# Gate and up products of a two-layer trunk as seven quadrant products on one Trainium2 core

## The chip, the core and the metric

The kernel runs on one core of a Trainium2 chip. The metric is the device time of one execution in microseconds. Before the change three runs gave 1435.06, 1439.13 and 1439.5 us, a median of 1439.13 us.

## What is computed

The reference is a decoder trunk of two layers with 512 tokens, width 1024 and float32 data. Each layer has a mixer (retention and a state space model in layer 0, differential attention in layer 1), then a feed-forward part and a gated embedding. The change is in the feed-forward part, which has 2816 hidden columns:

```python
def swiglu(h, w_gate, w_up, w_down):
    return (jax.nn.silu(h @ w_gate) * (h @ w_up)) @ w_down
```

It is called once per layer on the normalised `h` of 512 x 1024.

## The kernel before

The trunk is written through a framework that schedules the instructions at build time: a timeline model there fixes one order for each engine and puts in the semaphores. On the chip each engine then takes its instructions in that order, so one that waits holds up all behind it on its engine. Buffers come from pools; a new tile waits until an earlier tile's last reader has released a slot.

A float32 product is made of three products of parts in the format float32r. A cast on ScalarE writes the high part (`hi`, line 98), a subtraction on VectorE the low part (`lo`, line 101), and `mm3` (lines 120 to 122) adds hi x hi, hi x lo and lo x hi in PSUM. The normalised activations are kept transposed, as `xh` and `xl` of 128 x 8 x 512 (eight pieces of 128 rows of the width, 512 tokens).

`ffn` (from line 965) goes over 22 tiles of 128 hidden columns. For each it loads 1024 columns of gate and of up weights (`gu`, two DMAs of 512 KB), splits them into `whi` and `wlo`, and `gu_mm` makes 2 outputs x 8 pieces x 3 = 48 matmuls of 512 columns into two PSUM banks. Then ScalarE takes the silu of the gate bank (line 993), VectorE multiplies it with the up bank into `pr` (line 994), and a split gives `ah` and `al`. For the first two tiles the matmuls come in two halves of 256 columns, so that they can begin before all tokens are normalised. After `FA` = 12 tiles and after the last, the down product (`gemm_nat`, 512 columns) adds what these tiles give to the residual (`residual_evac`, line 245):

```python
            if ft in (FA - 1, NFT - 1):
                half = 0 if ft == FA - 1 else 1
                prs = range(6) if half == 0 else range(6, 11)
                nt = open_norm(i_out) if half else None
                for c in range(2):
                    gemm_nat(ah, al, [A["down"][L, c, i] for i in prs], [2] * len(prs),
                             residual_evac(i_out, c, half == 1, nt if c else None), t_outer=(half == 1 and c == 1))
```

The pools of `whi` and `wlo` have five slots each, that of the raw weights three. PSUM has six banks for products here.

Of the kernel before, what the change touches and what calls it, by code (L numbers as in the profile page):

```python
# [9 lines left out]
F32 = mybir.dt.float32  # L10
F32R = mybir.dt.float32r
BF16 = mybir.dt.bfloat16
I32 = mybir.dt.int32
AF = mybir.ActivationFunctionType
ALU = mybir.AluOpType
# [4 lines left out]
P = 128  # L20
D = 1024
S = 512
NT = S // P
KD = D // P
FH = 2816
NFT = FH // P
FA = 12
EPS = 1e-6
MAGIC = 12582912.0
TWO_PI = 2.0 * math.pi  # L30
# [36 lines left out]
def trunk(ctx: ExitStack, tc, A, out, stop=None, tap=None):  # L67
    nc = tc.nc
    V, G, AC, PE, SP = nc.vector, nc.gpsimd, nc.scalar, nc.tensor, nc.sync

    cpool = ctx.enter_context(tc.tile_pool(name="cpool", bufs=1))
    wpool = ctx.enter_context(tc.tile_pool(name="wpool", bufs=5))
    rpool = ctx.enter_context(tc.tile_pool(name="rpool", bufs=3))
# [12 lines left out]
    def f(t):  # L86
        return t.bitcast(F32)

    def bank(tag="mm"):
        r = rings[tag]  # L90
        n = r[0] + r[2] % r[1]
        r[2] += 1
        n, w = (f"b{n // 2}", 2) if n < 6 else (f"c{n}", 1)
        return psum.tile([P, 512], F32, tag=n, name=n, bufs=w)

    def split(hi, lo, src, hi_eng=AC, lo_eng=V):
        if hi_eng is AC:
            AC.copy(out=hi, in_=src)  # L98
        else:
            hi_eng.tensor_copy(out=hi, in_=src)  # L100
        lo_eng.tensor_tensor(out=lo, in0=src, in1=f(hi), op=ALU.subtract)  # L101
# [3 lines left out]
    def wload(ap, lo_eng=V, parts=1):  # L105
        if on_pool[0] > 0:
            on_pool[0] -= 1
            lo_eng = G
        raw = rpool.tile([P, 1024], F32, tag="raw", name="raw")
        hi = wpool.tile([P, 1024], F32R, tag="whi", name="whi")  # L110
        lo = wpool.tile([P, 1024], F32R, tag="wlo", name="wlo")
        w = 1024 // parts
        for i in range(parts):
            cs = slice(i * w, (i + 1) * w)
            SP.dma_start(out=raw[:, cs], in_=ap[:, cs])
            split(hi[:, cs], lo[:, cs], raw[:, cs], lo_eng=lo_eng)
# [41 lines left out]
    def norm_fn(i, gain, alloc, tr=lambda t: "tr"):  # L158
        def scaled(t):
            rstd_of(i, t)  # L160
            y = alloc()
            for c in range(2):
                V.scalar_tensor_tensor(out=y[c], in0=hold[0][:, t, c * 512:(c + 1) * 512], scalar=rst[:, i, t:t + 1],
                                       in1=gain[c], op0=ALU.mult, op1=ALU.mult)
            return y

        def norm_t(t):
            y = scaled(t)
            for c in range(2):
# [22 lines left out]
    def gemm_parts(xh, xl, pieces, kpp, evac, k0=0, lo_engs=(V,), last=(), ring="mm"):  # L192
        w = [wload(a, lo_engs[i % len(lo_engs)]) for i, a in enumerate(pieces)]
        wk = []
        for (hi, lo), n in zip(w, kpp):
            for j in range(n):
                wk.append((hi[:, j * 512:(j + 1) * 512], lo[:, j * 512:(j + 1) * 512]))
        n = len(wk)

        order = [k for k in range(n) if k not in last] + list(last)  # L200

        def part(t, ring=ring, *cols):
            b = bank(ring)
# [38 lines left out]
    def residual_evac(i, c, do_sq=True, after=None):  # L242
        def ev(t, b):
            hs = hold[0][:, t, c * 512:(c + 1) * 512]
            V.tensor_tensor(out=hs, in0=b, in1=hs, op=ALU.add)
            if do_sq:
                sumsq(i, t, c)
            if after is not None:
                after(t)
        return ev  # L250
# [702 lines left out]
    def gu(L, ft):  # L953
        return bank(), bank(), [wload(A["gateup"][L, ft, i]) for i in range(2)]

    def gu_mm(w, a, b):
        for o, (whi, wlo) in zip(w[:2], w[2]):
            for k in range(KD):
                cs = slice(k * P, (k + 1) * P)
                mm3(o[:, a:b], whi[:, cs], wlo[:, cs], xh[:, k, a:b], xl[:, k, a:b], k == 0, k == KD - 1)  # L960
# [8 lines left out]
    def ffn(L, i_in, i_out, pre=None):  # L969
        banks(mm=6, tr=2)  # L970
        st = ExitStack()
        fp = st.enter_context(tc.tile_pool(name=f"ffn{L}", bufs=1, side="right"))
        if pre is None:
            close_norm()
            first, rest = ffn_first(L, 0, 256), (256, 512)
        else:
            first, rest = pre, (0, 256)
            rings["mm"][2] = 4
        ah = al = None
        for ft in range(NFT):  # L980
            if ft in (0, FA):
                ah = fp.tile([P, FA, S], F32R, tag="ah", name="ah")
                al = fp.tile([P, FA, S], F32R, tag="al", name="al")
            if ft < 2:
                w = first[ft]
                gu_mm(w, *rest)
            else:
                w = gu(L, ft)
                gu_mm(w, 0, 512)
            gb, ub = w[:2]  # L990
            sg = fp.tile([P, 512], F32, tag="sg", name="sg", bufs=2)
            pr = fp.tile([P, 512], F32, tag="pr", name="pr", bufs=2)
            AC.activation(sg, gb, AF.Silu)
            V.tensor_tensor(out=pr, in0=ub, in1=sg, op=ALU.mult)  # L994
            fi = ft % FA
            split(ah[:, fi], al[:, fi], pr)
            if ft in (FA - 1, NFT - 1):
                half = 0 if ft == FA - 1 else 1
                prs = range(6) if half == 0 else range(6, 11)
                nt = open_norm(i_out) if half else None  # L1000
                for c in range(2):
                    gemm_nat(ah, al, [A["down"][L, c, i] for i in prs], [2] * len(prs),
                             residual_evac(i_out, c, half == 1, nt if c else None), t_outer=(half == 1 and c == 1))
        st.close()

    def ple(L, i_in, i_out):
# [171 lines left out]
```

## Time and profile before

| | before |
|---|---|
| median of three runs | 1439.13 us |
| the profiled execution | 1437.59 us |
| its span, first to last instruction | 1435.8 us |
| TensorE (PE) busy | 1382.5 us, 96% |
| VectorE (DVE) busy | 723.0 us, 50% |
| ScalarE (ACT) busy | 553.5 us, 39% |
| GpSimd (POOL) busy | 276.8 us, 19% |
| mean granted TensorE clock | 0.976 |
| HBM traffic over the span | 99 GB/s |

The profiled execution has its own time, 1437.59 us, which is 1.8 us above its span. Matmuls are pipelined, so the duration of one is longer than the distance from its start to the next start; a rate is read from starts. PEld is the load of the stationary operand, which runs beside PE. DVE, ACT and POOL rows have true starts, and the bracket at the end of a timeline row tells how long the engine was idle before it and who ended that.

### The profile page before, as it was taken

What the parts mean: (1) busy time and instruction counts of PE and PEld (TensorE: products, weight loads), DVE (VectorE), ACT (ScalarE), POOL (GpSimd) and SP (SyncE); (2) the same over time, 40 slices, a digit from 0 to 9 for tenths busy, and PEclk for the clock granted to TensorE, in tenths of its full rate; (3) what the DMA queues carried; (4) which work ended last, traced back from release to release, by engine and by line L of the source; (5) the groups of instructions that cost most, each with busy time, mean ns of one, the idle gap of its engine ahead of it and who ended that gap; (6) DMA issues with size and microseconds to landing.
All of it is one profiled execution on the core that took longest, in us unless ns stands there. A gap on an engine that the chain in (4) does not pass through costs nothing.

```text
span 1435.8 us, 17051 instructions
## 1 busy us (share of the span) xinstructions
PE 1382.5 (96%) x6538; PEld 1131.3 (79%) x6538; DVE 723.0 (50%) x1244; ACT 553.5 (39%) x956; POOL 276.8 (19%) x275
## 2 busy tenths in 40 slices
PE   7999887899999999999999999898999999999997
PEld 5788665689888888888888888787988888888886
DVE  7998565454333233333553777887533323333344
ACT  5335445443232222222544565864423212232244
POOL 0113463331000000000344364732100000000041
PEclk9999788999999999999999999999999999999999
DMA  7532125324323333231432332323333332323241
GB/s 255 159 99 83 48 68 160 117 64 129 102 88 99 92 91 100 89 101 61 151 124 77 104 86 55 100 81 103 118 96 96 90 101 88 102 90 91 85 147 59
DMA packets 48272, 145.28 MB, mean 101 GB/s; under 512 B 10752, under 2 KB 10896, under 8 KB 48192
## 3 DMA queue, kind: packets, MB, share of 16 engines
q1 hardware_dynamic: 43040, 136.37, 30.0%
q0 software_dynamic: 5008, 7.84, 2.3%
q8 instruction: 51, 0.84, 0.2%
q14 instruction: 29, 0.24, 0.1%
q10 hardware_dynamic: 144, 0.00, 0.0%
HBM read 133.21 MB, written 8.88 MB: 99 GB/s over the span
## 4 chain that ended last, share of the span: by engine, by line
PE 87%; DVE 6%; issue 3%; ACT 2%; DMA 2%; POOL 1%; SPq 0%; POOLq 0%; ACTq 0%; DVEq 0%
PE b L120 26%; PE b L121 26%; PE b L122 26%; DVE wlo L101 1%; PE c L172 1%; DVE T L404 1%; PE c L853 1%; PE b L831 1%; PE b L830 1%; PE c L583 1%; ACT whi L98 0%; PE b L844 0%; PE c L609 0%; DMA raw<-in_xT_dram 0%; PE b L781 0%
## 5 line engine op out<-in xcount | busy, mean ns | idle before, releaser
L98 ACT CAST whi<-raw 128x1024 fp32r<-128x1024 f32 (+1 forms) x217 | 226.4, 1045 | 540.5 <-PE b L121 316.5
L101 DVE TENSOR_TENSOR wlo<-raw,whi 128x1024 fp32r<-128x1024 f32 (+1 forms) x192 | 239.3, 1248 | 330.8 <-ACT whi L98 326.7
L120 PE MATMUL b<-xh,whi 128*128 128x512 f32 (+1 forms) x800 | 300.7, 378 | 5.3 <-ACT whi L98 5.3
L121 PE MATMUL b<-xl,whi 128*128 128x512 f32 (+1 forms) x800 | 301.3, 378 | 0.0
L122 PE MATMUL b<-xh,wlo 128*128 128x512 f32 (+1 forms) x800 | 299.2, 377 | 0.0
L120 PE MATMUL b<-whi,xh 128*128 128x512 f32 (+1 forms) x576 | 228.8, 403 | 14.8 <-ACT xh L98 8.6
L121 PE MATMUL b<-wlo,xh 128*128 128x512 f32 (+1 forms) x576 | 230.9, 403 | 3.2 <-DVE wlo L101 3.2
L122 PE MATMUL b<-whi,xl 128*128 128x512 f32 (+1 forms) x576 | 226.7, 399 | 0.0
L120 PEld LDWEIGHTS b<-xh,whi 128*128 128x128 f32 x800 | 150.6, 189 | 35.9 <-ACT whi L98 5.7
L121 PEld LDWEIGHTS b<-xl,whi 128*128 128x128 f32 x800 | 151.1, 189 | 30.2
L122 PEld LDWEIGHTS b<-xh,wlo 128*128 128x128 f32 x800 | 150.8, 189 | 30.2
L125 POOL TENSOR_TENSOR rst<-ms,mhalf 128x1 f32<-128x1 f32 (+1 forms) x25 | 14.9, 599 | 782.6 <-DVE ms L154 734.1
L120 PEld LDWEIGHTS b<-whi,xh 128*128 128x128 f32 x576 | 110.6, 192 | 41.0 <-ACT xh L98 9.1
L121 PE MATMUL b<-wlo,ah 128*128 128x512 f32 x352 | 139.2, 395 | 0.0
L122 PE MATMUL b<-whi,al 128*128 128x512 f32 x352 | 138.9, 395 | 0.0
L120 PE MATMUL b<-whi,ah 128*128 128x512 f32 x352 | 138.7, 395 | 0.0
L121 PEld LDWEIGHTS b<-wlo,xh 128*128 128x128 f32 x576 | 111.0, 193 | 28.1 <-DVE wlo L101 4.5
L122 PEld LDWEIGHTS b<-whi,xl 128*128 128x128 f32 x576 | 109.9, 191 | 22.8 <-issue 0.5
L994 DVE TENSOR_TENSOR pr<-b,sg 128x512 f32<-128x512 f32 x44 | 30.5, 692 | 152.3 <-PE b L122 142.7
L121 PEld LDWEIGHTS b<-wlo,ah 128*128 128x128 f32 x352 | 66.0, 187 | 16.1
L120 PEld LDWEIGHTS b<-whi,ah 128*128 128x128 f32 x352 | 66.0, 187 | 16.0
L122 PEld LDWEIGHTS b<-whi,al 128*128 128x128 f32 x352 | 66.0, 187 | 16.0
(291 smaller groups left out, 1684.2 us busy)
## 6 DMA issues: line engine op xcount, KB each, us to landing
raw<-in_gateup_dram SPq DMA_DIRECT2D x88, 512.0 KB, 3.5
raw<-in_down_dram SPq DMA_DIRECT2D x44, 512.0 KB, 3.5
raw<-in_w_qkv_dram SPq DMA_DIRECT2D x24, 512.0 KB, 3.7
raw<-in_w_in_dram SPq DMA_DIRECT2D x19, 512.0 KB, 4.3
raw<-in_ple_gate_dram SPq DMA_DIRECT2D x16, 512.0 KB, 3.6
pj<-raw SPq DMA_DIRECT2D x8, 512.0 KB, 2.9
raw<-in_w_out_dram SPq DMA_DIRECT2D x8, 512.0 KB, 4.2
pj<-pj SPq DMA_DIRECT2D x8, 512.0 KB, 6.6
```

The lines of the kernel that those rows point to most:

```text
L98: AC.copy(out=hi, in_=src)
L101: lo_eng.tensor_tensor(out=lo, in0=src, in1=f(hi), op=ALU.subtract)
L120: PE.matmul(o, lhsT=sh, rhs=mh, start=start, stop=False)
L121: PE.matmul(o, lhsT=sh, rhs=ml, start=False, stop=False)
L122: PE.matmul(o, lhsT=sl, rhs=mh, start=False, stop=stop)
L125: G.tensor_tensor(out=dst, in0=src, in1=mhalf[:, :w], op=ALU.pow)
L172: PE.transpose(out=b[:, j * P:(j + 1) * P], in_=y[c][:, j * P:(j + 1) * P], identity=ident)
L404: TT = lambda e, o, a, b, op: e.tensor_tensor(out=o, in0=a, in1=b, op=op)
L583: PE.matmul(vb[:, g * 64:(g + 1) * 64], lhsT=AT[:, g], rhs=U[:, g], start=True, stop=True)
L830: PE.matmul(so, lhsT=QQ[m][:, qs], rhs=KK[m][:, 0:n], start=True, stop=False)
L831: PE.matmul(so, lhsT=QQ[m][:, qs], rhs=KZ[m][:, 0:n], start=False, stop=True)
L994: V.tensor_tensor(out=pr, in0=ub, in1=sg, op=ALU.mult)
```

## The change

Tiles 0, 1 and 2 of each layer stay as they were. From tile 3 (`NORD` = 3) on, gate and up of a tile are computed as one product of two 2 x 2 block matrices, in Winograd's form of Strassen's algorithm. The token matrix is cut into two halves of 256 tokens and two halves of the width (`x11`, `x12`, `x21`, `x22`); the weights into gate and up (columns) and two halves of the width (`b11`, `b21`, `b12`, `b22`). Seven products of 4 pieces x 3 = 12 matmuls with 256 columns each take the place of the 48 with 512.

- `x_sums`, once per layer, makes the sums S1 to S4 of token quadrants: ten VectorE operations on 128 x 1024 and four splits. S3 is written over `x21`, which tiles 0 to 2 still read.
- `w_sums`, once per tile, makes four sums of weight quadrants (T1 to T4, 128 x 512 each) and splits the plain weights `w1`, the pairs `w2` (T1, T2) and `w4` (T4 and b22), each 128 x 1024, and `w3` (T3, 128 x 512).
- Running sums are kept in PSUM: three copies by ScalarE (`s1`, `u2`, `u3`) save what a bank half holds at that moment, and three VectorE operations on 128 x 256 add them in elsewhere.
- The last two of a tile's seven products (`d_gate`, `d_up`) are issued within the next tile's.
- The down product comes after 8, 16 and 22 tiles (8, 8 and 6) where it came after 12 and 22.

```diff
-FA = 12
+FA = 8
+NORD = 3
...
+        def x_sums():
...
+            tt(s12, f(x21[0]), f(x22[0]), ALU.add)
+            tt(s12, s12, f(x21[1]), ALU.add)
+            tt(s12, s12, f(x22[1]), ALU.add)
+            put("S1", s12)
+            tt(s12, s12, f(x11[0]), ALU.subtract)
+            tt(s12, s12, f(x11[1]), ALU.subtract)
+            put("S2", s12)
+            tt(s3, f(x11[0]), f(x21[0]), ALU.subtract)
+            tt(s3, s3, f(x11[1]), ALU.add)
+            tt(s3, s3, f(x21[1]), ALU.subtract)
+            s4 = quad(fp.tile([P, 1024], F32, tag="T", name="s4"))
+            tt(s4, f(x12[0]), s12, ALU.subtract)
+            tt(s4, s4, f(x12[1]), ALU.add)
+            put("S4", s4)
+            return lambda: put("S3", s3, x21)
+
+        def w_sums(ft):
+            r1 = rpool.tile([P, 1024], F32, tag="raw", name="raw")
+            r2 = r2_tile("r2")
+            for r, i in ((r1, 0), (r2, 1)):
+                SP.dma_start(out=r, in_=A["gateup"][L, ft, i])
+            T = fp.tile([P, 1536], F32, tag="T", name="T")
...
+            w1 = pair(r1, wt())
+            tt(t1, b12, b11, ALU.subtract)
+            tt(t2, b22, t1, ALU.subtract)
+            w2 = pair(T[:, 0:1024], wt())
+            tt(t3, b22, b12, ALU.subtract)
+            w3 = pair(t3, [fp.tile([P, 512], F32R, tag=n, name=n, bufs=2) for n in ("t3h", "t3l")])
+            tt(b12, b21, t2, ALU.subtract)
+            w4 = pair(r2, wt())
...
+        def prod(o, w, x, start):
+            for k in range(HK):
+                cs = slice(k * P, (k + 1) * P)
+                for i, (wi, xi) in enumerate(((0, 0), (1, 0), (0, 1))):
+                    PE.matmul(o, lhsT=w[wi][:, cs], rhs=x[xi][:, k], start=start and k == 0 and i == 0,
+                              stop=k == HK - 1 and i == 2, skip_group_check=True)
+
+        def snap(src, n):
+            d = fp.tile([P, HS], F32, tag=n, name=n, bufs=2)
+            AC.copy(out=d, in_=src)
+            return d
...
+            def d_gate():
+                prod(X, w["T4"], x22, False)
+
+            def d_up():
+                prod(Y, w["22"], xs["S4"], False)
+                tt(Y, s["u2"], Y, ALU.add)
+                evac(ft, gb, ub)
...
+        for ft in range(NFT + 1):
+            if ft < NORD:
...
+                if ft == 1:
+                    put_s3 = x_sums()
+                if ft == NORD - 1:
+                    put_s3()
+                continue
...
+                prod(X, w["11"], x11, True)
+                s1 = snap(X, "s1")
+                prod(Z, w["21"], x12, True)
+                tt(gb[:, 0:HS], s1, Z, ALU.add)
+                if pend:
+                    pend[0]()
+                prod(X, w["T2"], xs["S2"], False)
+                u2 = snap(X, "u2")
+                if pend:
+                    pend[1]()
+                prod(Y, w["T1"], xs["S1"], True)
+                prod(X, w["T3"], xs["S3"], False)
+                u3 = snap(X, "u3")
+                tt(Z, u3, Y, ALU.add)
+                pend = finish_ft(ft, w, gb, ub, {"u2": u2}, None)
+            if ft == NFT or ft % FA == 0:
+                down(ft - 1 - (ft - 1) % FA, ft)
```

Three places of the built order follow. First VectorE in the middle of the tiles, before the change: one tile has four instructions (its product `pr`, its low part `al` and the low parts `wlo` of two later weight loads; `b` is a PSUM bank, `sg` the silu).

```order
L994 TENSOR_TENSOR pr<-b_3133,sg 128x512
L101 TENSOR_TENSOR wlo<-raw,whi 128x1024
L101 TENSOR_TENSOR al<-pr,ah 128x512
L101 TENSOR_TENSOR wlo<-raw,whi 128x1024
L994 TENSOR_TENSOR pr<-b_3201,sg 128x512
```

The same place with the change. A tile has thirteen; here stand twelve that follow the first weight sum T1 of one tile. `r` holds the up weights, `s`, `u` are the copies from PSUM, and `t3l` is the low part of T3.

```order
L986 TENSOR_TENSOR T<-r_3555 128x512
L986 TENSOR_TENSOR T<-r_3555,T 128x512
L102 TENSOR_TENSOR wlo<-r_3429,whi 128x1024
L986 TENSOR_TENSOR r_3555<-raw,T 128x512
L986 TENSOR_TENSOR b_3202<-u_3254,b_3202 128x256
L102 TENSOR_TENSOR wlo<-raw,whi 128x1024
L986 TENSOR_TENSOR pr<-b_3202,sg 128x512
L986 TENSOR_TENSOR b_3328<-u_3425,b_3328 128x256
L102 TENSOR_TENSOR t3l<-T,t3h 128x512
L986 TENSOR_TENSOR b_3453<-s_3467,b_3454 128x256
L102 TENSOR_TENSOR al<-pr,ah 128x512
L102 TENSOR_TENSOR wlo<-T,whi 128x1024
```

The four instructions of a tile have become thirteen: three of 1024 columns, six of 512 between SBUF tiles, `pr`, and three of 256 in PSUM.

Second, VectorE of the changed kernel at the passage from tile 2 to tile 3 in layer 0. `xl<-s3` is the low part of S3, `pr_2948` belongs to tile 2, `wlo_2967` and `wlo_2977` are the pairs w2 and w4 of tile 3, `wlo_3056` the plain weights w1 of tile 4.

```order
L102 TENSOR_TENSOR xl_79<-s3_2861,xh_78 128x4x256
L986 TENSOR_TENSOR r2_2956<-raw_2955,T_2959 128x512
L102 TENSOR_TENSOR t3l_2972<-T_2959,t3h_2971 128x512
L986 TENSOR_TENSOR pr_2948<-b2_2886,sg_2947 128x512
L102 TENSOR_TENSOR wlo_2967<-T_2959,whi_2966 128x1024
L102 TENSOR_TENSOR wlo_2977<-r2_2956,whi_2976 128x1024
L102 TENSOR_TENSOR wlo_3056<-raw_3050,whi_3055 128x1024
```

Six instructions, among them the low parts that TensorE needs next, stand behind the low part of S3. In layer 1 ten stand between it and the low part of w2 there.

Third, TensorE of the changed kernel at the same place, with its waits: the end of the second product of tile 3, then the first matmuls of tile 4.

```order
L1046 MATMUL b0_2981<-xl_79,whi_2960 128x256
L1046 MATMUL b1_3075<-xh_78,whi_3055 128x256 [waits PE_49,Activation_49]
L1046 MATMUL b1_3076<-xh_78,whi_3055 128x256 [waits DVE_49]
L1046 MATMUL b1_3075<-xh_78,wlo_3056 128x256 [waits DVE_49]
```

The 26 matmuls up to there (24 of tile 3, two of tile 4) need the plain weights alone; the next one waits for VectorE's `wlo_3056`.

## Rows read from the trace of the kernel before

**Rows 1.** The page: busy time by engine, and the chain that ended last.
```profile
PE 1382.5 (96%) x6538; PEld 1131.3 (79%) x6538; DVE 723.0 (50%) x1244; ACT 553.5 (39%) x956; POOL 276.8 (19%) x275
...
PE 87%; DVE 6%; issue 3%; ACT 2%; DMA 2%; POOL 1%; SPq 0%; POOLq 0%; ACTq 0%; DVEq 0%
```
**Rows 2.** Busy time by stretch: us; PE, PEld, DVE, ACT, POOL; clock; DMA share; GB/s.
```profile
400.00:450.00 50.00, 50.00 (x217) 40.55 (x216) 17.50 (x19) 14.43 (x18) 0.00 (x0) 1.00 0.31 95
450.00:500.00 50.00, 50.00 (x216) 40.23 (x215) 15.10 (x15) 10.53 (x11) 0.00 (x0) 1.00 0.30 87
```
**Rows 3.** Timeline of DVE over one tile: start us, duration us, what, idle before.
```profile
367.02 0.69 DVE L994 TENSOR_TENSOR pr<-b,sg 128x512 f32<-128x512 f32 x1 [3.52 <-PE b L122]
367.80 1.23 DVE L101 TENSOR_TENSOR wlo<-raw,whi 128x1024 fp32r<-128x1024 f32 x1
368.94 0.69 DVE L101 TENSOR_TENSOR al<-pr,ah 128x512 fp32r<-128x512 f32 x1
373.43 1.23 DVE L101 TENSOR_TENSOR wlo<-raw,whi 128x1024 fp32r<-128x1024 f32 x1 [3.80 <-ACT whi L98]
378.18 0.69 DVE L994 TENSOR_TENSOR pr<-b,sg 128x512 f32<-128x512 f32 x1 [3.52 <-PE b L122]
```
**Rows 4.** Timeline of PE in tile 1's half of 256 columns, twenty starts apart.
```profile
338.63 0.28 PE L122 MATMUL b<-xh,wlo 128*128 128x256 f32 x1
...
341.01 0.28 PE L121 MATMUL b<-xl,whi 128*128 128x256 f32 x1
```
**Rows 5.** Timeline of PEld in the same stretch.
```profile
338.52 0.19 PEld L122 LDWEIGHTS b<-xh,wlo 128*128 128x128 f32 x1
338.64 0.19 PEld L120 LDWEIGHTS b<-xh,whi 128*128 128x128 f32 x1
```
**Rows 6.** Groups by line, 300 to 690 us: count, busy us, mean ns, idle before.
```profile
L101 DVE TENSOR_TENSOR wlo<-raw,whi 128x1024 fp32r<-128x1024 f32 x60 | 73.5, 1225 | 141.5 <-ACT whi L98 139.7
L98 ACT CAST whi<-raw 128x1024 fp32r<-128x1024 f32 x67 | 70.3, 1050 | 241.9 <-PE b L121 155.6 <-PE b L122 67.3 <-issue 9.4
...
L994 DVE TENSOR_TENSOR pr<-b,sg 128x512 f32<-128x512 f32 x22 | 15.2, 692 | 80.2 <-PE b L122 71.2 <-ACT sg L993 9.0
L101 DVE TENSOR_TENSOR al<-pr,ah 128x512 fp32r<-128x512 f32 x22 | 15.1, 685 | 0.0
...
L98 ACT CAST ah<-pr 128x512 fp32r<-128x512 f32 x22 | 13.7, 621 | 0.0
...
L993 ACT ACTIVATE sg<-b 128x512 f32<-128x512 f32 x22 | 13.0, 592 | 0.0
```
**Rows 7.** Groups by line, 800 to 1000 us: 256 columns out of PSUM.
```profile
L857 DVE TENSOR_TENSOR vn<-c,vn 128x256 f32<-128x256 f32 x16 | 6.7, 418 | 8.8 <-ACT vn L856 8.8
...
L856 ACT COPY vn<-c 128x256 f32<-128x256 f32 x16 | 5.9, 369 | 16.4 <-PE c L854 16.4
```
**Rows 8.** Timeline of DVE where its instructions stand close, 93 to 107 us.
```profile
93.95 1.22 DVE L101 TENSOR_TENSOR wlo<-raw,whi 128x1024 fp32r<-128x1024 f32 x1
95.08 1.22 DVE L404 TENSOR_TENSOR Am<-BA,LM 128x1024 f32<-128x1024 f32 x1
...
105.42 0.68 DVE L404 TENSOR_TENSOR E<-bh,c 128x512 f32<-128x512 f32 x1
106.03 0.68 DVE L101 TENSOR_TENSOR vl<-b,vh 128x512 fp32r<-128x512 f32 x1
106.63 0.47 DVE L238 SCALAR_TENSOR_TENSOR rt<-b,rst,c 128x256 f32<-128x256 f32 x1
107.02 0.47 DVE L239 SCALAR_TENSOR_TENSOR rt<-b,rst,c 128x256 f32<-128x256 f32 x1
```
**Rows 9.** Timeline of DVE: the product `pr` of tile 2, layer 0 and layer 1.
```profile
355.87 0.69 DVE L994 TENSOR_TENSOR pr<-b,sg 128x512 f32<-128x512 f32 x1 [3.52 <-PE b L122]
...
1044.69 0.69 DVE L994 TENSOR_TENSOR pr<-b,sg 128x512 f32<-128x512 f32 x1 [3.57 <-PE b L122]
```
**Rows 10.** Busy time by stretch around a pause of PE in layer 0's mixer.
```profile
264.00:270.00 6.00, 2.69 (x11) 1.57 (x9) 5.56 (x5) 4.86 (x6) 5.96 (x4) 1.00 0.15 25
270.00:280.00 10.00, 7.93 (x28) 6.25 (x29) 6.24 (x6) 3.58 (x6) 2.61 (x2) 0.66 0.73 252
```

More of the change, by code (lines that the diff above doesn't have):

```diff
@@ L978, in ffn @@
             rings["mm"][2] = 4
[L979 to L986, printed above, removed]
-            else:
[L988 to L1003, printed above, removed]
@@ new lines, in ffn, with tt, r2_tile, put @@
+        HK, HS = KD // 2, S // 2
+        lo_t, hi_t = slice(0, HS), slice(HS, S)
+        x11, x12, x21, x22 = ([x[:, a:a + HK, t] for x in (xh, xl)] for t in (lo_t, hi_t) for a in (0, HK))
+        xs = {}
+        def tt(o, a, b, op):
+            V.tensor_tensor(out=o, in0=a, in1=b, op=op)
+        def r2_tile(name):
+            return fp.tile([P, 1024], F32, tag="r2", name=name, bufs=2)
+        def x_sums():
+            quad = lambda x: x.rearrange("p (k n) -> p k n", k=HK)
+            def put(n, src, dst=None):
+                if dst is None:
+                    dst = [fp.tile([P, HK, HS], F32R, tag=f"{n}{i}", name=f"{n}{i}") for i in "hl"]
+                split(dst[0], dst[1], src)
+                xs[n] = dst
+            s12, s3 = quad(r2_tile("s12")), quad(r2_tile("s3"))
+            tt(s12, f(x21[0]), f(x22[0]), ALU.add)
[13 more added lines that the diff above has]
+            return lambda: put("S3", s3, x21)
@@ new lines, in w_sums, with pair @@
+        def w_sums(ft):
[4 more added lines that the diff above has]
+            T = fp.tile([P, 1536], F32, tag="T", name="T")
+            t1, t2, t3 = (T[:, i * 512:(i + 1) * 512] for i in range(3))
+            b11, b21, b12, b22 = r1[:, 0:512], r1[:, 512:], r2[:, 0:512], r2[:, 512:]
+            def pair(src, new):
+                hi, lo = new
+                split(hi, lo, src)
+                return hi, lo
+            wt = lambda: [wpool.tile([P, 1024], F32R, tag=n, name=n) for n in ("whi", "wlo")]
+            w1 = pair(r1, wt())
[6 more added lines that the diff above has]
+            w4 = pair(r2, wt())
+            half = lambda w, i: [x[:, i * 512:(i + 1) * 512] for x in w]
+            return {"11": half(w1, 0), "21": half(w1, 1), "T1": half(w2, 0), "T2": half(w2, 1), "T3": w3,
+                    "T4": half(w4, 0), "22": half(w4, 1)}
@@ new lines, in ffn, with evac, down @@
+        ahl = [None, None]
+        def evac(ft, gb, ub):
+            if ft % FA == 0:
+                ahl[:] = [fp.tile([P, FA, S], F32R, tag=n, name=n) for n in ("ah", "al")]
+            sg = fp.tile([P, 512], F32, tag="sg", name="sg", bufs=2)
+            pr = fp.tile([P, 512], F32, tag="pr", name="pr")
+            AC.activation(sg, gb, AF.Silu)
+            tt(pr, ub, sg, ALU.mult)
+            split(ahl[0][:, ft % FA], ahl[1][:, ft % FA], pr)
+        def down(n0, n1):
+            last = n1 == NFT
+            prs = range(n0 // 2, n1 // 2)
+            nt = open_norm(i_out) if last else None
+            for c in range(2):
+                gemm_nat(ahl[0], ahl[1], [A["down"][L, c, i] for i in prs], [2] * len(prs),
+                         residual_evac(i_out, c, last, nt if c and last else None), t_outer=(last and c == 1))
@@ new lines, in finish_ft @@
+        def finish_ft(ft, w, gb, ub, s, z):
+            X, Y = gb[:, HS:], ub[:, 0:HS]
+            def d_gate():
[4 more added lines that the diff above has]
+                evac(ft, gb, ub)
+            return d_gate, d_up
+        pend = None
+        for ft in range(NFT + 1):
+            if ft < NORD:
+                w = first[ft] if ft < 2 else gu(L, ft)
+                gu_mm(w, *(rest if ft < 2 else (0, 512)))
+                evac(ft, *w[:2])
+                if ft == 1:
[3 more added lines that the diff above has]
+                continue
+            if ft == NFT:
+                pend[0]()
+                pend[1]()
+            else:
+                w = w_sums(ft)
+                gb, ub = bank(), bank()
+                X, Y, Z = gb[:, HS:], ub[:, 0:HS], ub[:, HS:]
+                prod(X, w["11"], x11, True)
[3 more added lines that the diff above has]
+                if pend:
+                    pend[0]()
+                prod(X, w["T2"], xs["S2"], False)
+                u2 = snap(X, "u2")
+                if pend:
+                    pend[1]()
+                prod(Y, w["T1"], xs["S1"], True)
[5 more added lines that the diff above has]
+                down(ft - 1 - (ft - 1) % FA, ft)
```

## The prediction

> **What bounds the kernel now.** I read the page first: PE is busy 96% of the span, and 87% of the chain that ended last is PE work [rows 1]. That average hides stages, so I read the stretches next. In the feed-forward part PE is busy in all of the 50 us between 400 and 450, at a granted clock of 1.00 (the 2.4 GHz level), while VectorE is busy 17.5 and ScalarE 14.4; during the down product, 450 to 500, it is the same picture [rows 2]. So here time is matmuls, and the other engines have room. The timeline of VectorE gives the beat: from one `pr` to the next, which waits for PE, it is 378.18 - 367.02 = 11.16 us a tile [rows 3]. With 48 matmuls in a tile, one of 512 columns takes 232 ns.
>
> **TensorE, the part that is removed.** From tile 3 on a tile has 7 x 12 = 84 matmuls of 256 columns. The first two tiles already contain such halves, each with its own weight load, with hi and lo weights in turn as the new ones: twenty starts take 341.01 - 338.63 = 2.38 us, so 119 ns each [rows 4]. That is a little over half of 232, so halving the columns loses 3%, and 84 x 119 = 10.0 us stand against 11.16. The change saves 1.16 us on 19 tiles of 2 layers: 38 x 1.16 = 44 us. Its bounds come from the digits of the two starts (118.5 to 119.5 ns), 42 to 46 us.
>
> A weight load lasts 0.19 us, and loads start 0.12 us apart while matmuls run [rows 5], so they overlap and do not set the pace. The Trainium skill (TensorE: Matmul & The Clock Gate, "The mechanism") says that a load overlaps matmuls in flight only when its row group differs, which would not be so here, where each load fills all rows. The trace contradicts it. What it would cost is a rival below.
>
> **The down product.** Its matmuls only change their grouping. There are eight more residual additions a layer, of about the length of `pr`, 0.69 us [rows 6]. They lie on VectorE beside PE's down matmuls, where VectorE is busy 15.1 of 50 us [rows 2], and cost nothing; without that cover they would cost 16 x 0.69 = 11 us. The DMAs move the same bytes in the same pieces.
>
> **VectorE and ScalarE in a middle tile.** VectorE goes from four instructions a tile to thirteen: three of 1024, six of 512, `pr`, three of 256 in PSUM. With full durations, 1225, 685, 692 [rows 6] and 418 ns [rows 7], that is 3.7 + 4.1 + 0.7 + 1.25 = 9.7 us. But instructions that stand close start earlier than the former ends: 1.13 us apart at 1024, 0.61 at 512, 0.39 at 256 [rows 8], and 0.78 behind `pr` [rows 3]. By starts it is 3.4 + 3.65 + 0.78 + 1.2 = 9.0 us. I take the starts, since that is how a full queue runs, so VectorE fills 90% of PE's 10.0 us. ScalarE gets one cast of 1024, one of 512 and three copies of 256 more: 1.05 + 0.62 [rows 6] + 3 x 0.37 [rows 7] = 2.8 us on 14.4 x 11.16 / 50 = 3.2 [rows 2], 6.0 of 10.0. Neither sets the pace, if its queue is not held up. I followed the order by hand from tile 3 to tile 7: each sum and low part is there before PE's first matmul that reads it, most by under 2 us. Nothing in the old trace shows such tight handovers. Their cost lies between 0 and one product (12 x 119 ns = 1.43 us) lost in every second tile, 27 us in all; I take 3 us, near the lower end, because the hand count found none.
>
> **The start of the new tiles, the part that is added on the path.** S3 is written over quadrant `x21`, so its split must wait until tile 2's last matmul has ended, which is where `pr` of tile 2 stands: 355.87 in layer 0 and 1044.69 in layer 1 [rows 9]. All that VectorE has behind it waits too. Layer 0: silu 0.59 and cast 1.05 [rows 6] bring us to 357.5; the low part of S3, 1.13, to 358.6; one sum and the low part of T3 to 359.9; `pr` to 360.6; three low parts of 1024 to 364.0. That last one is what PE needs after 26 matmuls of 119 ns, at 359.0. So PE waits 5 us. Layer 1: cast 1.05, low part 1.13, then six of 512, `pr`, one of 256 (4.8 us) and the low part of w2 end at 1052.8; PE needs that after 28 matmuls, at 1048.0, and waits 5 us too, and perhaps 2 more for the first weights of tile 5, whose low part comes twelve places further on in VectorE's order. I take 5 + 7 = 12 us; the ends are 0, if the queue is further ahead than I think, and twice that.
>
> A pause of this length also costs clock. After 264 to 270, where PE was busy only 2.7 of 6 us, the granted clock of the next 10 us averaged 0.66, with PE busy in 7.9 [rows 10]. At the lower level (1.2 GHz) a stretch does half its work, so up to 3.4 us are lost; I take 2 a layer, between 0 and 3.4, as PE here comes back with dense work.
>
> **Sum.** The profiled execution took 1437.6 us: 1437.6 - 44 + 12 + 4 + 3 = 1412.6. That execution lies 1.5 us below the median of the runs shown, and I predict 1413. The unknown terms at their ends give 1400 (start hidden, no further waits) and 1440; the middle, where two of three come out as taken, is 1404 to 1424.
>
> **The rivals.**
> - *The start is hidden* (chance 0.10). If the S sums and splits leave PE no wait, the 16 us go: 1397. For it speaks that most of the S sums can be made while PE works on tiles 0 to 2; against it, that S3 cannot be written before tile 2 has ended.
> - *VectorE sets the pace of the middle tiles* (0.14). Every handover that comes late adds to 9.0. At 10.5 us a tile the time is 1413 + 38 x 0.5 = 1432, still faster. For it speaks the thin margin; against it, the starts of neighbours, which overlap [rows 8]. [...]
> - *Slower, through ScalarE's queue* (0.12). Three copies out of PSUM a tile wait for a product of PE, and the casts behind them on ScalarE wait with them; VectorE waits for the cast, PE for VectorE. If the queue is so held once a tile for one product, 1.43 us, the tile takes 11.4 us and the kernel 1413 + 38 x 1.43 = 1467. It decides from 0.69 us a tile on, where the remaining gain of 26 us is gone. For it: one order for all engines, fixed at build time with other durations than the chip's. Against it: ScalarE is 60% busy, and each copy is due at least one whole product before its bank half is written again.
> - *Weight loads do not overlap* (0.01). Then a matmul would start after the former's 0.28 us [rows 4]: 84 x 0.28 = 23.5 us a tile, and 1413 + 38 x 13.5 = 1926. Rows 4 and 5 show the opposite.
> - *The change does not do what it says* (0.01): 1439. The built order has 84 matmuls of 256 columns in a tile, which all but excludes it.
>
> **How the numbers follow.** My forecast has 0.62. A measurement of this kernel can tell about 0.3%, 4.3 us, from no change. The forecast, the hidden start and most of VectorE's pace are faster by more: 0.62 + 0.10 + 0.10 = 0.82. Within 0.3% lie the rest of VectorE's pace and the change without effect: 0.05. Slower: 0.13 with the loads. The range leaves out ScalarE's queue and the worst of VectorE's pace: 1396 to 1434.
>
> **What would show it.** Right: in the middle tiles the starts of `pr` are 10.0 us apart on average, PE is busy all of it at clock 1.00, and VectorE about 90%; once a layer, just behind tile 2, PE waits about 5 us for `wlo`. Wrong: PE idle in every tile, ended by VectorE (its pace) or VectorE idle in every tile, ended by ScalarE's casts (the queue), or starts of 256-column matmuls further apart than 119 ns.

## The result and the profile after

The changed kernel takes 1403.34 us (median of 4 runs, 1399.21 to 1405.62) against 1439.32 us before: a ratio of 0.9746, 95% interval 0.9707 to 0.9785. The prediction was 1413 with a range of 1396 to 1434. Sign and bound were right, but the gain, 36 us, is nearly 40% larger than the 26 that the forecast makes against the 1439.13 us before.

The profiled execution took 1405.62 us, with a span of 1403.8. First the page's busy times and its chain; they answer to [rows 1].

```profile
PE 1343.2 (96%) x7906; PEld 1171.0 (83%) x7906; DVE 960.0 (68%) x1630; ACT 662.9 (47%) x1154; POOL 278.2 (20%) x275
...
PE 41%; DVE 4%; issue 1%; ACT 1%; POOL 0%; POOLq 0%; ACTq 0%; DVEq 0%
```

PE has 1368 matmuls more (38 tiles x 36) and is busy 39 us less. VectorE has 237 us more to do and is still at 68%. The chain covers less than half of the span here, so it says little.

Busy time by stretch (columns as in [rows 2]): a stretch with the end of a down product, one with new tiles, and the passage from the old to the new tiles with the 5 us behind it.

```profile
450.00:500.00 50.00, 50.00 (x349) 46.47 (x348) 36.20 (x52) 22.93 (x33) 0.00 (x0) 1.00 0.27 85
...
500.00:550.00 50.00, 49.83 (x402) 48.77 (x402) 39.44 (x57) 27.01 (x42) 0.00 (x0) 1.00 0.34 106
...
360.00:370.00 10.00, 7.98 (x61) 7.44 (x60) 10.00 (x15) 5.61 (x9) 0.00 (x0) 1.00 0.48 157
...
370.00:375.00 5.00, 4.26 (x36) 4.05 (x36) 5.00 (x8) 3.69 (x6) 0.00 (x0) 1.00 0.57 157
```

In the tiles PE is busy all but 0.17 of 50 us at a granted clock of 1.00, as forecast; VectorE is at 39.4 of 50, less than the 90% forecast (19 of the 402 matmuls here already belong to the next down product). From 496.04 to 536.22, over four tiles, `pr` starts 10.05 us apart on average, as forecast. Only at the passage, 360 to 370, is it the other way round: VectorE 10.00 of 10, PE 7.98.

What PE waits for in the feed-forward part (us in total, times, longest), layer 0 (310 to 690 us) and then layer 1 (950 to 1370):

```profile
PE b L1046 <- DVE wlo L102: 2.0, 1, 2.0
PE b L1046 <- DVE b L986: 0.7, 1, 0.7
PE b L1046 <- ACT u L1051: 0.2, 1, 0.2
```

```profile
PE b L1046 <- ACT whi L99: 2.5, 2, 1.3
...
PE b L1046 <- DVE wlo L102: 1.0, 1, 1.0
PE b L1046 <- ACT u L1051: 0.3, 2, 0.2
```

That is 2.9 and 3.8 us, 6.7 in all, where the prediction had 12 for the start and 3 for other handovers. (L102 is now the low part's line, L986 that of a sum, L1046 that of the seven products, L1051 that of a copy from PSUM.)

To see where the time went I measured the feed-forward part alone, from the start of the first gate matmul to the start of the last down matmul. These are the two ends in layer 0, from the timeline of PE (start us, us, ...):

```profile
324.99 0.40 PE L121 MATMUL b<-xh,whi 128*128 128x256 f32 x2
...
678.13 0.40 PE L123 MATMUL b<-whi,al 128*128 128x512 f32 x1
```

The part went from 373.17 to 353.14 us in layer 0 (-20.0) and from 378.63 to 360.44 in layer 1 (-18.2). Everything else together became 6 us longer in these two profiled executions. That is mostly the mixer of layer 0, which the change does not touch: the part begins at 319.51 us before and at 324.99 after. The run *down8* below, whose mixer is the old one too, begins it at 322.88, and all the kernels below at 318 to 326. So this is variation between executions, and the table gives the parts beside the medians. Each part is from one profiled execution; the changed kernel's two differ by 0.03 us in layer 0 and 0.25 in layer 1.

| kernel | median us | ratio to before, 95% | part begins at | layer 0 part | layer 1 part |
|---|---|---|---|---|---|
| before | 1438.5 to 1439.4 | 1 | 319.5 | 373.2 | 378.6 |
| changed | 1403.34 | 0.9707 to 0.9785 | 325.0 | 353.1 | 360.4 |
| changed, run again (*control*) | 1402.26 | 0.9695 to 0.9748 | 323.0 | 353.2 | 360.2 |
| *korder* | 1401.89 | 0.9724 to 0.9771 | 322.0 | 351.8 | 358.4 |
| *klate* | 1401.30 | 0.9718 to 0.9756 | 318.4 | 352.5 | 359.8 |
| *nord4* | 1395.38 | 0.9679 to 0.9719 | 322.3 | 350.8 | 356.6 |
| *nord2* | 1416.37 | 0.9816 to 0.9867 | 322.9 | 358.7 | 365.9 |
| *s4x2* | 1412.26 | 0.9788 to 0.9844 | 319.9 | 355.5 | 362.6 |
| *relief* | 1406.48 | 0.9747 to 0.9800 | 325.8 | 354.2 | 363.6 |
| *s1v* | 1408.18 | 0.9735 to 0.9797 | 326.3 | 354.8 | 360.0 |
| *down8* | 1439.22 | 0.9982 to 1.0013 | 322.9 | 372.4 | 377.7 |
| *no_t3* | 1346.31 | 0.9336 to 0.9383 | 319.8 | 326.6 | 332.9 |
| *dve1* | 1404.21 | 0.9722 to 0.9784 | 323.9 | 354.3 | 361.0 |
| *dve3* | 1411.53 | 0.9781 to 0.9838 | 317.8 | 357.7 | 365.2 |

### The profile page after: what moved, and what is told of

Same layout as the page of the kernel before. It is cut to its first block, busy times and chain, and to the rows that moved or that the text cites. A ratio compares the mean times of both kernels' runs of the same rounds, so it can differ in the third digit from the quotient of the medians.

```text
span 1403.8 us, 20412 instructions
## 1 busy us (share of the span) xinstructions
PE 1343.2 (96%) x7906; PEld 1171.0 (83%) x7906; DVE 960.0 (68%) x1630; ACT 662.9 (47%) x1154; POOL 278.2 (20%) x275
## 5 line engine op out<-in xcount | busy, mean ns | idle before, releaser
L99 ACT CAST whi<-raw 128x1024 fp32r<-128x1024 f32 (+1 forms) x179 | 186.5, 1045 | 229.2 <-PE b L1046 96.9
L102 DVE TENSOR_TENSOR wlo<-raw,whi 128x1024 fp32r<-128x1024 f32 (+1 forms) x154 | 192.2, 1251 | 72.7 <-ACT whi L99 72.2
L102 POOL TENSOR_TENSOR wlo<-raw,whi 128x1024 fp32r<-128x1024 f32 x25 | 63.8, 2560 | 721.1 <-ACT whi L99 720.7
L1046 PE MATMUL b<-xh,wlo 128*128 128x256 f32 x456 | 127.3, 283 | 3.0 <-DVE wlo L102 3.0
L1046 PE MATMUL b<-xl,whi 128*128 128x256 f32 x456 | 127.6, 283 | 0.0
L1046 PE MATMUL b<-xh,whi 128*128 128x256 f32 x456 | 123.8, 283 | 1.7 <-ACT whi L99 1.2
L246 DVE TENSOR_TENSOR h<-b,h 128x512 f32<-128x512 f32 x70 | 47.6, 688 | 85.3 <-PE b L123 85.1
L1046 PEld LDWEIGHTS b<-xh,wlo 128*128 128x128 f32 x456 | 86.0, 189 | 4.1 <-DVE wlo L102 3.4
L1046 PEld LDWEIGHTS b<-xh,whi 128*128 128x128 f32 x456 | 84.1, 189 | 3.8 <-ACT whi L99 1.4
L1046 PEld LDWEIGHTS b<-xl,whi 128*128 128x128 f32 x456 | 86.1, 189 | 0.0
```

The costliest lines, as they stand in the source:

```text
L1046: PE.matmul(o, lhsT=w[wi][:, cs], rhs=x[xi][:, k], start=start and k == 0 and i == 0, stop=k == HK - 1 and i == 2, skip_group_check=True)
```

## Experiments: what sets the pace of the middle tiles

**down8.** The kernel before, with only the regrouping of down.

```diff
-FA = 12
+FA = 8
-            if ft in (0, FA):
+            if ft % FA == 0:
-            if ft in (FA - 1, NFT - 1):
+            if ft % FA == FA - 1 or ft == NFT - 1:
...
+                prs = range((ft - ft % FA) // 2, (ft + 1) // 2)
```

> The kernel before with one part of the change alone: down in groups of 8, 8 and 6 tiles in place of 12 and 10. Theory: the 16 additional residual additions (0.69 us each) lie beside PE's down matmuls and cost nothing: 1439 us within 3. Rivals: without that cover up to 11 us slower (1450); or the regrouping is a part of the gain, then 1430 or below.

Measured: 0.9997 of before (0.9982 to 1.0013), parts 0.7 and 0.9 us shorter. The regrouping costs nothing and brings nothing that can be told in the time; the gain is the seven products'.

**no_t3.**

```diff
-                prod(X, w["T3"], xs["S3"], False)
```

> The changed kernel without the product of T3 and S3 in each new tile (12 of 84 matmuls left out, its sums and splits still made). It shows what paces a tile when PE has only 72 x 119 ns = 8.6 us of work. Theory (PE sets the pace of the changed kernel, VectorE needs 9.0 us a tile by starts): 38 x 1.0 = 38 us less than the changed kernel, 1365. If VectorE needs 9.7 us (full durations): 11 us less, 1392. If it is quicker than 8.6: 54 us less, 1349. Rival (VectorE or its handovers already pace the changed kernel): 0 to 4 us less.

Measured: 1346.3 us, 56 less than the control, and the two parts 26.6 and 27.3 us shorter. The 12 matmuls left out, 38 x 12 x 0.119 = 54 us, come back whole. So PE's columns alone set the pace of the changed kernel's middle tiles, and VectorE follows even at 8.5 us a tile (72 matmuls of 0.1186 us): my 9.0 was too long. One stretch of this kernel (columns as above):

```profile
450.00:500.00 50.00, 50.00 (x399) 48.81 (x398) 48.51 (x72) 31.94 (x49) 0.00 (x0) 1.00 0.36 118
```

Here VectorE is nearly full, 48.51 of 50, and PE still has no gap.

**dve1 and dve3.** More work for VectorE in each new tile, with one and three additional instructions.

```diff
-            tt(t3, b22, b12, ALU.subtract)
+            for _ in range(2):      # dve3: range(4)
+                tt(t3, b22, b12, ALU.subtract)
```

> The changed kernel with the 512-element sum of T3 made twice in each new tile: one more VectorE instruction, 0.60 us by starts. Theory (PE paces, VectorE has 10% of room): VectorE goes to 9.6 of 10.0 us, the time rises by 0 to 5 us. Rival (VectorE paces): 38 x 0.60 = 23 us more, 1426.

> The changed kernel with the 512-element sum of T3 made four times in each new tile: three more VectorE instructions, 1.8 us by starts. Theory: VectorE at 9.0 + 1.8 = 10.8 us is past PE's 10.0, so the time rises by 38 x 0.8 = 30 us, 1433. By full durations (9.7 + 3 x 0.685 = 11.75) 38 x 1.75 = 66 us more, 1470. Rival (VectorE paces already): 38 x 1.8 = 68 us more. Rival (VectorE needs far less than 9.0): under 10 us more.

Measured: 1404.2 and 1411.5 us; the parts grow by 1.1 and 0.8 us with one, by 4.5 and 5.0 with three. One more is free within what can be told. Three do not fit any more, but cost 9.3 us, a third of the 30 expected. Two things make the difference. VectorE's own starts in the changed kernel are closer than I took them, as this stretch of its timeline shows:

```profile
472.26 0.69 DVE L102 TENSOR_TENSOR al<-pr,ah 128x512 fp32r<-128x512 f32 x1
472.86 0.69 DVE L102 TENSOR_TENSOR t3l<-T,t3h 128x512 fp32r<-128x512 f32 x1
473.46 0.42 DVE L986 TENSOR_TENSOR b<-s,b 128x256 f32<-128x256 f32 x1
473.79 0.68 DVE L986 TENSOR_TENSOR r<-raw,T 128x512 f32<-128x512 f32 x1
474.39 1.22 DVE L102 TENSOR_TENSOR wlo<-T,whi 128x1024 fp32r<-128x1024 f32 x1
475.53 0.42 DVE L986 TENSOR_TENSOR b<-s,b 128x256 f32<-128x256 f32 x1
```

0.60 us behind 512, 0.33 behind 256, 1.14 behind 1024: a tile is 3 x 1.14 + 6 x 0.60 + 0.60 + 3 x 0.33 = 8.6 us. With three more it is 10.4 against PE's 9.96, 0.45 x 19 = 8.6 us a layer. Of these 4.5 to 5.0 show; that VectorE builds up a lead during the three down products of a layer, where PE needs little of it, would explain the rest, and this was not tried alone. In *dve3* PE is busy 48.51 of the 50 us from 500 to 550 (49.83 without the additional work), and its waits there are put down to ScalarE's copies `u`.

## Experiments: what PE waits for at the passage

**control, korder, klate.** The prediction had S3 wait for the end of tile 2. The trace after shows otherwise. The timelines of ScalarE, of VectorE and of PE at the passage in layer 0:

```profile
358.46 1.05 ACT L99 CAST xh<-s 128x1024 fp32r<-128x1024 f32 x1 [1.03 <-PE b L123]
```

```profile
356.97 1.23 DVE L102 TENSOR_TENSOR S4l<-s,S4h 128x1024 fp32r<-128x1024 f32 x1 [1.11 <-ACT S4h L99]
358.23 0.69 DVE L986 TENSOR_TENSOR T<-r,raw 128x512 f32<-128x512 f32 x1
358.84 0.69 DVE L986 TENSOR_TENSOR T<-r 128x512 f32<-128x512 f32 x1
359.44 0.69 DVE L986 TENSOR_TENSOR T<-r,T 128x512 f32<-128x512 f32 x1
360.04 1.22 DVE L102 TENSOR_TENSOR xl<-s,xh 128x1024 fp32r<-128x1024 f32 x1
361.18 0.69 DVE L986 TENSOR_TENSOR r<-raw,T 128x512 f32<-128x512 f32 x1
361.78 0.69 DVE L102 TENSOR_TENSOR t3l<-T,t3h 128x512 fp32r<-128x512 f32 x1
362.38 0.69 DVE L986 TENSOR_TENSOR pr<-b,sg 128x512 f32<-128x512 f32 x1
362.98 1.22 DVE L102 TENSOR_TENSOR wlo<-T,whi 128x1024 fp32r<-128x1024 f32 x1
364.12 1.22 DVE L102 TENSOR_TENSOR wlo<-r,whi 128x1024 fp32r<-128x1024 f32 x1
365.25 1.22 DVE L102 TENSOR_TENSOR wlo<-raw,whi 128x1024 fp32r<-128x1024 f32 x1
```

```profile
360.81 0.40 PE L123 MATMUL b<-xh,wlo 128*128 128x512 f32 x1
...
366.52 0.39 PE L1046 MATMUL b<-xh,wlo 128*128 128x256 f32 x1 [2.02 <-DVE wlo L102]
```

The high part of S3 is cast at 358.46, while tile 2 runs on until 361.0. The quadrant `x21` is pieces 0 to 3 of the width, and tile 2's up product reads these in its first half; the 12 matmuls behind them, 12 x 0.233 = 2.8 us, need pieces 4 to 7. The order of the seven VectorE instructions is the one the prediction read, and so is the one PE waits for, the last. That they begin earlier by the 2.8 us would make the wait 5.0 - 2.8 = 2.2, measured 2.02. But the agreement does not show that the release binds: the cast had ended at 359.51, S3's low part starts at 360.04, and VectorE works without a gap from S4's low part on, for whose cast it had last been idle. To see whether the release itself sets the wait I moved it both ways, by the order in which tile 2 takes its pieces.

```diff
+                    for ks in (range(HK), range(HK, KD)):     # korder
+                        for o, (whi, wlo) in zip(w[:2], w[2]):
+                            for k in ks:
...
+                    for o, (whi, wlo) in zip(w[:2], w[2]):    # klate
+                        for k in (4, 5, 6, 7, 0, 1, 2, 3):
```

> The changed kernel as it is, beside the other three on the same chip. 1403 us, plus or minus 4. In layer 0's feed-forward part the PE waits about 2.0 us for wlo just behind tile 2, in layer 1's about 3.8 us in all (2.5 for casts, 1.0 for wlo); if mixer 0's extra 5.5 us in the profile of the changed kernel is variation between executions, the first gate matmul of layer 0 starts at 319 to 325 us here and moves without any edit.

> Tile 2 reads pieces 0 to 3 for gate and up first, then pieces 4 to 7, so the last matmul that reads x21 stands 24 matmuls (5.6 us) before the tile's end rather than 12 (2.8 us). Theory (what PE waits for at tile 3 is set by the moment x21 is released to S3): the 2.0 us wait for wlo in layer 0 goes, layer 1's 3.8 us shrink to 1.5 or less, 2 to 4 us less than the control in all, read from the two profiles' waits. Rival (VectorE's backlog of S1, S2 and S4 sets it, not the release): waits of 2.0 and 3.8 us as in the control, time the same within 1 us.

> Tile 2 reads pieces 4 to 7 first and 0 to 3 last, for gate and for up, so x21 is released with the tile's last matmul, as the prediction assumed. Theory (the release sets the wait): layer 0's wait for wlo grows from 2.0 to about 4.8 us, layer 1's in all from 3.8 to about 6.5; 5 to 6 us more than the control. Rival (backlog): as the control within 1 us.

Measured: *control* repeats the waits of 2.0 and 3.8 us to the tenth. *korder* has 1.6 and 2.4 us, and its parts are 1.3 and 1.8 us shorter, though its median is the control's; as its VectorE in layer 0 takes S3's low part (355.09) ahead of the three sums `T` (from 356.22), it changed the order too and decides nothing alone. *klate* speaks against the theory: with the release at the very end the parts are not 2.8 us longer but 0.7 and 0.4 shorter, and layer 0's wait for `wlo` is 1.2. Its VectorE says why, in layer 0:

```profile
355.44 1.22 DVE L102 TENSOR_TENSOR wlo<-T,whi 128x1024 fp32r<-128x1024 f32 x1
356.57 1.22 DVE L102 TENSOR_TENSOR wlo<-r,whi 128x1024 fp32r<-128x1024 f32 x1
357.71 1.22 DVE L102 TENSOR_TENSOR wlo<-raw,whi 128x1024 fp32r<-128x1024 f32 x1
358.84 1.22 DVE L102 TENSOR_TENSOR xl<-s,xh 128x1024 fp32r<-128x1024 f32 x1
```

The order of instructions is made when the kernel is built, and with the later release it put S3's low part (`xl<-s`) behind the three low parts of weights. PE needs those first, and S3 only at the end of tile 3. So in layer 0 the release is not what PE waits for; it is VectorE's queue, and what stands in it ahead of the weights. In layer 1 *klate* still has S3's low part ahead of the three (1027.46), and its waits are 2.8 us against 3.8; most of that, 2.4, is put down to a weight DMA. As an experiment on the release alone *klate* failed, since it changed two things.

Layer 1 of the changed kernel has a second cause. Of its 3.8 us of waits 2.5 are for casts by ScalarE, and there a copy from PSUM stood 3.12 us waiting for a product of PE, with the casts behind it:

```profile
1031.33 0.37 ACT L1051 COPY s<-b 128x256 f32<-128x256 f32 x1 [3.12 <-PE b L1046]
...
1032.64 1.04 ACT L99 CAST whi<-T 128x1024 fp32r<-128x1024 f32 x1
```

VectorE's sum for that cast was ready at 1032.06. So these waits are partly VectorE's queue and partly ScalarE's order, the form that the rival of ScalarE's queue feared in every tile; how they divide was not measured.

**nord4, nord2, s4x2.** The queue's length, by the time it is given and by the work in it.

```diff
-NORD = 3
+NORD = 4                      # nord2: NORD = 2
...
-            tt(s4, f(x12[0]), s12, ALU.subtract)
+            for _ in range(3):      # s4x2 alone
+                tt(s4, f(x12[0]), s12, ALU.subtract)
```

> One more tile a layer in the old form (48 x 232 ns) ahead of the new ones. It costs 2 x 1.16 = 2.3 us of columns. Theory: with one more tile of time (11 us) VectorE is done with S1, S2 and S4 before S3 is released, and little of the 5.8 us of waits stays: 1 to 3 us less than the control. Rival (the release of x21 by the last old tile sets the wait, wherever that tile stands): the waits stay as they are, 2.3 us more than the control.

> One tile a layer fewer in the old form: the new tiles begin at tile 2. Theory (the waits at the passage are VectorE's queue: S sums, their splits and the first weights have to be made in the time of the old tiles): 2 x 1.25 = 2.5 us of columns go, but VectorE loses a cover of 11.2 us a layer, of which the run with one more old tile shows that 3 to 5 us would have been to spare; PE waits 6 to 9 us more a layer than in the control, and the kernel takes 1412 to 1418. Rival (what is late is the release of x21 alone): the same waits as in the control, 1400.

> The first sum of S4 (1024 elements, 1.13 us by starts) made three times: 2.27 us more on VectorE once a layer, behind S2 and ahead of the first weights of the new tiles. Theory (VectorE's queue): 2 x 2.3 = 4 to 5 us more than the control, 1406 to 1407, as more wait of PE in the first two new tiles; up to 2 us less than that if the order on VectorE changes with it. Rival (release of x21): the same as the control, 1402.

Measured: with one old tile more all that is left of the waits in layer 0 is

```profile
PE b L1046 <- ACT u L1051: 0.2, 1, 0.2
```

and the same 0.2 in layer 1. The parts are 2.4 and 3.6 us shorter in spite of the additional columns, and the kernel takes 1395.4 us. Of the kernels that leave nothing out it is the quickest. Its median lies 7 us below the control's, its ratio to before 0.0022, some 3 us, below (0.9699 against 0.9721, and the intervals overlap); the two parts, 6.0 us shorter in sum, are the clearer sign. The release stands at the end of the last old tile here too, so by the release alone the waits would have stayed. In layer 0 the order changed as well (S3's low part comes behind the weights' low parts, at 370.36), but the tile also gave VectorE room: it stood idle 2.77 us ahead of 369.15.

With one old tile fewer the time is 1416.4 us, within the 1412 to 1418 expected, though not by waits alone. Layer 0's wait, what stood behind it, and busy time by stretch around it:

```profile
PE b L1046 <- ACT whi L99: 6.7, 1, 6.7
```

S3's low part on VectorE, and ScalarE's cast just ahead of the one that PE waits for:

```profile
348.06 1.22 DVE L102 TENSOR_TENSOR xl<-s,xh 128x1024 fp32r<-128x1024 f32 x1
```

```profile
355.58 0.62 ACT L99 CAST t3h<-T 128x512 fp32r<-128x512 f32 x1 [3.49 <-DVE T L986]
```

```profile
350.00:355.00 5.00, 0.64 (x6) 0.43 (x4) 4.97 (x7) 1.58 (x2) 0.00 (x0) 0.79 0.62 210
355.00:360.00 5.00, 2.13 (x8) 1.84 (x9) 4.96 (x7) 3.56 (x4) 0.00 (x0) 0.50 0.29 107
360.00:365.00 5.00, 5.00 (x32) 5.00 (x32) 5.00 (x7) 3.02 (x5) 0.00 (x0) 0.69 0.36 115
```

VectorE is full there, PE almost empty. The wait is put down to a cast, but ScalarE had itself waited 3.49 us for VectorE's sum; and S3's low part was done at 349.28, 8 us before PE went on, so its release is not what PE waited for. Behind PE's pause the granted clock is 0.50, the 1.2 GHz level; it is 0.69 from 360 to 365 and 1.00 in the next 5 us. Waits grow by 4.5 and 5.9 us a layer, less than the 6 to 9 expected; the parts are 5.5 and 5.7 us longer although 1.23 us of columns a layer are gone. That leaves 2.2 us in layer 0 and 1.0 in layer 1 for the clock, by the difference.

In *s4x2* the parts grow by 2.3 and 2.4 us, as expected by size, but not in the form expected: the waits grow by only 0.5 and 0.2 us, since the order on VectorE changed as well. The rest I put down to the clock, which is lower behind the waits here and is 1.00 in the changed kernel:

```profile
360.00:365.00 5.00, 2.92 (x16) 2.72 (x17) 5.00 (x8) 2.42 (x4) 0.00 (x0) 0.84 0.41 125
365.00:370.00 5.00, 5.00 (x38) 5.00 (x38) 5.00 (x6) 3.96 (x6) 0.00 (x0) 0.82 0.47 153
```

Its median is 10 us above the control's, more than its parts explain. I count it as inconclusive for the queue: more work there costs time, but not as the theory has it.

**relief and s1v.** Two ways to shorten VectorE's queue: low parts of weights on GpSimd, and S1's cast by VectorE where it stood idle for ScalarE (layer 0 alone).

```diff
-        on_pool[0] = 6 if L == 0 else 4
+        on_pool[0] = 6
...
-            w1 = pair(r1, wt())
+            w1 = pair(r1, wt(), G if ft == NORD else V)
...
-                split(dst[0], dst[1], src)
+                split(dst[0], dst[1], src, hi_eng=V if n == "S1" and L == 0 else AC)   # s1v alone
```

> Low parts of weights moved from VectorE to GpSimd: of the first weight block of tile 3 in both layers, and of both blocks of tile 2 in layer 1 (layer 0 has those on GpSimd already). VectorE has 1.13 us less to do in layer 0 and 3.4 in layer 1 ahead of the passage; on GpSimd one takes 2.56 us. Theory (VectorE's queue): layer 0's wait falls from 2.0 to about 0.9 us, layer 1's 3.8 us to at most 1.5; 2 to 4 us less than the control, 1398 to 1400. Rival: GpSimd's 2.56 us come too late, PE waits for wlo from GpSimd, and the time is the control's or more.

> In layer 0 the high part of S1 is cast by VectorE itself, where it stood idle 3.1 us for ScalarE's cast; layer 1 is as in the changed kernel. Theory (VectorE's queue, without a gap from there to the new tiles, sets layer 0's wait): VectorE loses about 1.2 us to the cast, or less, and gains 3.1, so it is 1.9 us or more ahead, and layer 0's 2.0 us for wlo falls to under 0.5; its feed-forward part takes 351 to 352 us in place of 353.2; layer 1 stays at 360. Rival (release of x21 by tile 2, or something else behind it): wait and part as in the control.

Measured: both fail. *relief* has waits of 2.6 and 5.3 us (control 2.9 and 3.8) and parts 1.0 and 3.4 us longer than the control; *s1v* has a part 1.6 us longer in layer 0, with a wait of 3.1 us for `wlo` in place of 2.0. PE never waits for GpSimd, as the rival would have it. What was to be won is lost on VectorE; its timelines in *s1v* and then in *relief*, each with GpSimd's row of that moment:

```profile
343.56 0.69 DVE L101 CAST S1h<-s 128x1024 fp32r<-128x1024 f32 x1
344.28 3.31 DVE L102 TENSOR_TENSOR S1l<-s,S1h 128x1024 fp32r<-128x1024 f32 x1
```

```profile
343.94 2.57 POOL L102 TENSOR_TENSOR wlo<-raw,whi 128x1024 fp32r<-128x1024 f32 x1 [10.45 <-ACT whi L99]
```

```profile
347.90 2.82 DVE L986 TENSOR_TENSOR s<-s,xh 128x1024 f32<-128x1024 f32 x1
```

```profile
347.14 2.49 POOL L102 TENSOR_TENSOR wlo<-raw,whi 128x1024 fp32r<-128x1024 f32 x1 [1.39 <-ACT whi L99]
```

A subtraction that takes 1.22 us elsewhere takes 3.31 here, and a sum 2.82: each starts while GpSimd is at a low part, and ends 1.08 us after GpSimd's has ended (347.59 - 346.51; 350.72 - 349.63 = 1.09), as if it had begun only then. In *s1v* this gives back nearly all that the cast, at 0.69 us, had won; and its order put the weights' last low part behind two sums more, 1.2 us, which makes the wait longer than the control's. In *relief* VectorE saves 1.13 us in layer 0 and loses 1.6. The waits do not account for the longer parts: in layer 0 they are 3.3 us in *s1v* and 2.6 in *relief*, against the control's 2.9, and of *relief*'s 3.4 us in layer 1 they make 1.5. The rest I put down to the clock: behind PE's wait of 3.1 us *s1v* has, and behind one of 2.1 us *relief* has

```profile
370.00:375.00 5.00, 5.00 (x32) 5.00 (x31) 5.00 (x8) 2.64 (x4) 0.00 (x0) 0.66 0.39 121
```

```profile
370.00:375.00 5.00, 5.00 (x34) 5.00 (x34) 3.80 (x6) 3.80 (x5) 0.00 (x0) 0.73 0.26 83
```

where the changed kernel, behind its wait of 2.0, shows 1.00 throughout. In layer 1 both *control* and *s1v* have two waits close together, 2.5 us in sum; *control* shows 1.00 there and behind them (1030 to 1040), *s1v* 0.75 (1040 to 1045). So the length of a wait alone does not decide what it costs in clock. Neither run tells what a queue shortened without such a clash would give; that stays open.

## Why the prediction was right, and where it was off

- **The part that is removed, 44 us**: right in mechanism, a little small. Over the neighbouring starts in the last 345 us of layer 0's part, pauses left out, a matmul of 512 columns takes 0.2332 us and one of 256 takes 0.1186: 48 x 0.2332 - 84 x 0.1186 = 1.23 us a tile, 47 us for 38. *no_t3* shows that these columns are the pace. That is 1 us above the bound of 46 that the prediction gave. The rounding of two starts in [rows 4] and of one `pr` to the next in [rows 3] hid the 3 us.
- **Weight loads**: they overlap as the prediction read [rows 5]; 402 loads in 50 us go beside 402 matmuls.
- **The down product at nothing**: shown by *down8*.
- **VectorE at 9.0 us a tile**: 8.6 by the starts in the changed kernel; the 0.39 of [rows 8] belonged to another operation, and the 0.78 of [rows 3] to one `pr` that had waited. The margin was 1.35 us, not 1.0. The rivals of VectorE's pace and of ScalarE's queue did not come: one more VectorE instruction a tile is free, and the waits on ScalarE's copies are 0.5 us in both layers together. Only at layer 1's passage did ScalarE's order cost PE something.
- **The start, 12 us**: this is the term that was mis-sized. The step that failed is "S3 is written over quadrant `x21`, so its split must wait until tile 2's last matmul has ended". The split waits only for the last matmul that reads `x21`, 2.8 us earlier, and in layer 0 even the release is not the binding event, but VectorE's queue: VectorE has no gap there, *klate*'s later release, with the order changed, made no longer wait, and in *nord2* PE waits 6.7 us with S3's low part long done. Measured: 2.7 us in layer 0 and 3.5 in layer 1 as waits for VectorE's results and ScalarE's casts. *nord4* takes nearly all of it away, *nord2* makes it 2 to 3 times as long.
- **The clock, 4 us**: nothing here; the granted clock stays at 1.00 behind the passage. The mechanism exists, as *nord2* and *s1v* show behind pauses of 6.7 and 3.1 us. The pause was taken too long, but that alone does not explain the 1.00: *relief* fell to 0.73 behind one of 2.1 us. Why the changed kernel keeps its clock stays open.
- **Other handovers, 3 us**: 0.5 us as ScalarE's copies.

Put together: -47 for the columns and +8.4 for all pauses (the 6.7 of waits, and smaller ones that show only as gaps between starts) are -39; the two parts measured are -38.2. The profiled execution shows only -32 because its mixer took longer; the medians show -36. The forecast's terms erred on one side, so nothing cancelled: 3 us too little saved, 11 too much lost (12 + 4 + 3 = 19 against the 8.4). The 1403 us lie nearer to the 1397 of the hidden start than to the forecast's 1413, and the start is neither hidden nor as long as forecast. Two ends of the prediction's sum are also wrong as they stand: by its own terms no loss at all gives 1437.6 - 44 = 1394, not 1400, and all losses at their most give 1437.6 - 44 + 24 + 6.8 + 27 = 1451, not 1440.

## What to carry to other kernels

When a change hands work to an engine with room on average, look at the one place where its queue must be full of preparation: here PE waits nearly nowhere in the feed-forward part but at the passage, and one more old tile as cover (*nord4*) made the two parts 6 us shorter although that tile itself costs more. Read the release of a buffer from the last instruction that reads that piece of it, not from the end of the tile. And an edit that moves one dependency may move the built order as well, so an experiment of a few us is read from the timeline before it is read from the median.

## What was not expected of the hardware

VectorE instructions of 1024 columns with two inputs in SBUF that start during a GpSimd subtraction ended 1.08 to 1.09 us after it, in the three cases at the passages of *relief* and *s1v* (3.31, 2.82 and, in *relief*'s layer 1, 3.31 us in place of 1.22). The trace of the kernel before has such cases too, so the price could have been read ahead of the two runs: GpSimd's low part ends at 1012.52, VectorE's at 1013.60.

```profile
1010.11 2.41 POOL L101 TENSOR_TENSOR wlo<-raw,whi 128x1024 fp32r<-128x1024 f32 x1 [3.43 <-ACT whi L98]
```

```profile
1011.47 2.13 DVE L101 TENSOR_TENSOR wlo<-raw,whi 128x1024 fp32r<-128x1024 f32 x1 [0.39 <-ACT whi L98]
```

The Trainium skill (SBUF — State Buffer, "SBUF: two separate sides") has the two engines share one pair of ports, which the first to start holds for its whole instruction; these rows agree. Moving work from VectorE to GpSimd is therefore no relief by the length of the work moved. A cast of 1024 columns took VectorE 0.69 us, against 1.05 on ScalarE [rows 6].
